# The branch to the general path is moved ahead of the last expert's last column group, and the planner restores its places after a skipped path

## The chip, the cores and the metric

The kernel runs on one core of a Trainium2 chip. The metric is the device time of one execution in microseconds (us). A core has TensorE (PE, matmuls; its weight loads are shown as PEld), VectorE (DVE), ScalarE (ACT), GpSimd (POOL) and SyncE (SP), each with its own instruction stream that it works through in order. Here SP issues nearly all transfers from HBM, and POOL does nothing but the branch.

## What is computed

A transformer of four layers on 256 tokens of width 1024, in float32. The first block has a convolution layer with a dense feed-forward, and an attention layer with a mixture of experts; the second block has two hybrid layers (three attention branches, the third over a memory `mem_2`) with an MLP each. The change lies in the mixture of experts and at the beginning of the first hybrid layer.

```python
def moe_swiglu(h, router, we_gate, we_up, we_down):
    logits = (h @ router).astype(jnp.float32)
    top_v, top_i = lax.top_k(logits, TOP_K)                  # 2 of 8 experts for each token
    ...
    for e in range(N_EXPERTS):
        out = out + gates[..., e:e + 1] * swiglu(h, we_gate[e], we_up[e], we_down[e])
    return out

def memory_attn(q, mem_n, w_mkv):
    kv = (mem_n @ w_mkv).reshape(B, M, 2, N_HEADS_M, HEAD_DIM)
    ...
```

## The kernel before

**Recording and planning.** The kernel's code does not issue instructions. It records them (`Recorder.add`), and `Recorder.flush` plans all that was recorded since the flush before and issues it. `issue` keeps a clock for each engine and for SP's queue, and picks at each step the instruction that could start first, by priority; loads have a large negative bias, so they come as early as a place for their tile is free. An engine's stream is fixed by this plan: if an instruction must wait on the chip for longer than the plan has it, all behind it on that engine waits too. All instructions therefore have the line of `op.fn` in the profile (L694 before, L695 after the change).

**Places.** SBUF has 28 "large" places (4 KB of each partition: weight tiles and their halves), 38 "gen" places (2 KB) and 20 small ones; PSUM has 8 banks. `Places.free` holds, in the planner's time, when each place is free, and `drop` sets it when a tile's last use is planned. What an instruction on the chip really waits for are semaphores, set by the tile framework from the program's text: the user before it of the same place. PE, ACT and DVE count their instructions up in a semaphore each, and SP's transfers share eight semaphores in turn, so at most eight are under way.

**The experts.** `route` gives each token its two experts and a position in each expert's list. The fast path has room for 96 tokens (`CAP`, three `BLOCKS` of 32) an expert. `experts()` goes over 32 steps, 8 experts with 4 column groups each. A step has `proj` (gate and up projections: tiles of `e_in`, 16 a step, 8 in the last group, which is half as wide), `act` (silu on ACT, product and transpose on DVE), and `down` of the step before (tiles of `e_down`, 8 a step, 4 for the last group). A tile is 128x1024 float32, 512 KB, and has 12 matmuls, which PE shows as 24 records. After an expert's last `down`, `scatter` adds its result to the activations `xT`: ACT and DVE split it in two halves, 12 pieces each, PE does 16 matmuls, DVE adds four tiles to `xT`.

**The branch.** `moe` (L1317) records all 32 steps and the load of the first two `c0_qk` weight tiles (`AHEAD`), holds what is still needed, and flushes. Then it loads the largest list length `most` into a register of every engine (L1326) and opens two nested branches (L1327 to L1331). In them all experts are gone over again for tokens beyond 96 and beyond 192, with a flush of their own. With these inputs no list is longer than 96, so the path is skipped: each engine compares, jumps, and adds to its semaphores what the skipped path would have added. `flush(aside=True)` sets the planner's engine clocks back, and lets no place be free later than the latest engine clock before the branch.

**Behind the branch** come, in one last flush: the scatter of expert 7; `fill(200)`, which runs `mem_second(1)`, the keys and values of `mem_2` for the second hybrid layer (4 tiles of `mem2T`, 2 of `c1_mk`, 2 of `c1_mv`; ACT squares and scales `mem2T`, PE does 16 matmuls of 128x256 in float32 for the keys and 16 for the values); the first hybrid layer `hybrid(0)`, whose first matmuls take `xT` and the 12 tiles of `c0_qk`, each split in two halves by ACT and DVE; and all the rest of the kernel.

Of the kernel before, what the change touches and what calls it, by code (L numbers as in the profile page):

```python
# [37 lines left out]
LATE = True  # L38
ATT_BIAS = 0
EARLY = 6  # L40
AHEAD = 1
LOAD_SHIFT = 0
Q_BIAS = 20e3
MEM1_BIAS = 20e3
MEM_AT = 2, 200
GATHER_AT = 1
GATES = 2
MEM_BIAS = (0, 0)
LOAD_FIRST = 1e9
SPLIT_LEAD = 5e3  # L50
# [290 lines left out]
class Recorder:  # L341
# [152 lines left out]
    def flush(self, aside=False):  # L494

        before = dict(self.free)
        ops, self.ops = self.ops, []
        if not ops:
            return
        self.issue(ops)  # L500
        if aside:
            self.free = before
            top = max(before.values())
            for op in ops:
                op.end = min(op.end, top)
            for c in self.kinds.values():
                for p in c.places:
                    p.free = [v if v is None else min(v, top) for v in p.free]
                for t in c.tiles:
                    t.end = min(t.end, top)  # L510

# [185 lines left out]
class Net:  # L697
# [493 lines left out]
    def down(self, acc, w, hh, hl, first, last):  # L1191
        for m in range(8):
            ms = slice(m * 128, (m + 1) * 128)
            for i, (wh, wl) in enumerate(w):
                self.mm3(acc[m // 2][:, (m % 2) * S:(m % 2 + 1) * S], (wh[:, 0, ms], wl[:, 0, ms]),
                         (hh[:, i], hl[:, i]), first and i == 0 and m % 2 == 0, last and i == 1, skip=True)
# [119 lines left out]

    def moe(self):  # L1317

        self.route()
        back, y = self.experts()  # L1320
        self.ahead = [self.load(self.a["c0_qk"][0, u]) for u in range(AHEAD)]
        held = [t for j in self.xn for p in j for t in p] + [self.pos, self.gate, back, y[0], y[2]]
        self.nc.hold(held)
        self.nc.hold([t for w in self.ahead for p in w for t in p])
        self.nc.flush()
        most = self.tc.nc.values_load(self.most[0:1, 0:1], min_val=0, max_val=S)  # L1326
        with ExitStack() as inner:  # L1327
            for base in range(CAP, S, CAP):
                inner.enter_context(self.tc.If(most > base))
                self.scatter(*self.experts(float(base)))  # L1330
                self.nc.flush(aside=True)  # L1331
        self.scatter(back, y)
        self.nc.release(held)
        self.fill(200)

    def onehot(self, e, base):
# [72 lines left out]
    def experts(self, base=0.0):  # L1409

        nc, a = self.nc, self.a
        steps = [(e, g) for e in range(NE) for g in range(GROUPS)]
        G, B, Y, T = {}, {}, {}, {}

        def prepare(e):
            oh = self.onehot(e, base)
            got = self.gather(oh)
            for i in range(2):
                G[e + i] = got[i]
                B[e + i] = self.back(oh, i, e + i)  # L1420

        def four(out, at, x, w, start, stop):
            for j in range(4):
                nc.tensor.matmul(out[32 * j:32 * j + 32, at:at + 256], x, w[:, 256 * j:256 * j + 256], start=start,
                                 stop=stop, skip_group_check=True)

        def proj(s):
            e, g = s
            p = [self.mm() for _ in range(BLOCKS)]
            for k in range(KT):  # L1430
                at = [48 + k] if g == GROUPS - 1 else [(g * KT + k) * 2, (g * KT + k) * 2 + 1]
                ws = [self.tile_of(a["e_in"][e, n]) for n in at]
                for b in range(BLOCKS):
                    for m, w in enumerate(ws):
                        four(p[b], m * 256, G[e][k][:, 32 * b:32 * b + 32], w, k == 0 and m == 0, k == KT - 1)
            return p

        def act(s, p):
            w = 128 if s[1] == GROUPS - 1 else 256
            T[s] = []  # L1440
            for b in range(BLOCKS):
                g = self.t([128, 256], F32, "eg")[:, :w]
                nc.scalar.activation(g, p[b][:, :w], AF.Silu)
                nc.vector.scalar_tensor_tensor(g, p[b][:, w:2 * w], B[s[0]][1][:, b:b + 1], g, op0=OP.mult, op1=OP.mult)
                t = self.t([128, 256], F32, "eh")
                nc.vector.transpose(t[:, :w], g)
                T[s].append(t)

        def down(s):
            e, g = s  # L1450
            if g == 0:
                y = [self.acc("y0"), self.acc("y1")]
                Y[e] = [y[0], y[0], y[1]]
            n = 4 if g == GROUPS - 1 else 8
            t = T.pop(s)
            for c in range(n):
                w = self.tile_of(a["e_down"][e, 8 * g + c])
                for b in range(BLOCKS):
                    four(Y[e][b], b % 2 * 256, t[b][:, 32 * c:32 * c + 32], w, g == 0 and c == 0 and b != 1,
                         g == GROUPS - 1 and c == n - 1)  # L1460
            if g < GROUPS - 1:
                return None
            y = Y.pop(e)
            return B.pop(e)[0], [y[b][:, b % 2 * 256:b % 2 * 256 + 256] for b in range(BLOCKS)]

        prepare(0)
        if not base:
            self.fill(2)
        for n, s in enumerate(steps):
            if not base:  # L1470
                self.fill(100 + n)
            act(s, proj(s))
            if n and (done := down(steps[n - 1])):
                self.scatter(*done)
            if s[1] == GATHER_AT and s[0] % 2 and s[0] + 1 < NE:
                prepare(s[0] + 1)
        return down(steps[-1])


    def fill(self, at):  # L1480
# [36 lines left out]
    def hybrid(self, l):  # L1517
        nc, a = self.nc, self.a
        f = self.feed(self.xT, "mix_g", l * 8)
# [4 lines left out]
        for c in range(3):  # L1524
            ps = [self.mm(), self.mm()]
            for u in range(2):
                if self.ahead:
                    w = self.ahead.pop(0)
                    self.nat(ps, f, w, 4 * u)
                    nc.release([t for p in w for t in p])  # L1530
                    continue
                w = self.load(a[f"c{l}_qk"][c, u])
                self.nat(ps, f, w, 4 * u)
            z = [self.t([128, 512], F32, f"z{j}") for j in range(2)]
# [20 lines left out]
        ps = [self.mm(), self.mm()]  # L1555
        for u in range(2):
            w = self.load(a[f"c{l}_v0"][0, u])
# [3 lines left out]
        w = self.load(a[f"c{l}_v1"])  # L1561
        p = self.mm()
# [3 lines left out]
        w = self.load(a[f"c{l}_qm"][0])  # L1566
        p = self.mm()
# [32 lines left out]
        kT, v = self.m2[l]  # L1600
# [5 lines left out]
        for mp in range(4):  # L1606
            w = self.load(a[f"c{l}_p"][mp])
            pp = []
            for ks in ([0], [1, 2, 3], [4, 5]):
                p = self.mm()  # L1610
                self.ws(p, w, ot, ks)
                pp.append(p)
            y = self.t([128, 2, S], F32, "y")
            t = self.t([128, 2, S], F32, "yt")
# [87 lines left out]
```

## Time and profile before

| | |
|---|---|
| three runs | 2177.43, 2179.4, 2180.08 us (median 2179.4) |
| profiled execution | 2182.62 us, its span 2180.8 us |
| PE busy | 2141.2 us, 98% of the span |
| DVE, ACT busy | 965.8 and 734.0 us |
| experts | about 440 to 1371 us |
| PE at the branch | 1370.1 us |

A timeline row has the start, the length, the engine, the instruction and in brackets the idle time before it with what ended it. A tile is named by its place (large, gen, bank) on the left of the arrow and by what is read on the right. A row of windows has the stretch, its length, each engine's busy time and number of instructions, the granted clock of PE (1 is full speed), the share of time that the transfer engines were busy, and GB/s. "Busy" on PE is modelled in parts, so idle time is taken from the gaps.

### The profile page before, as it was taken

How to read it: one execution, taken by the hardware profiler on the slowest of the kernel's cores; microseconds unless marked ns; L12 is line 12 of the kernel's file. 1: busy time of each engine (PE TensorE's matmuls, PEld its weight loads, DVE VectorE, ACT ScalarE, POOL GpSimd, SP SyncE). 2: the span in 40 equal slices, each digit the busy share in tenths (PEclk: the TensorE clock that was granted, in tenths of full speed). 3: DMA queues.
4: the chain of work that ended last, by engine and by line, in shares of the span. 5: the costliest groups of instructions: out<-in, count | busy, mean ns of one | idle time of the engine just before them, and what ended most of it. 6: DMA issues, size and time to landing. Idle time of an engine off the chain costs nothing. (4 is left out here: it accounts for less than half of the span.)

```text
span 2180.8 us, 57477 instructions
## 1 busy us (share of the span) xinstructions
PE 2141.2 (98%) x25496; PEld 1688.3 (77%) x25496; DVE 965.8 (44%) x2079; ACT 734.0 (34%) x1315; POOL 0.2 (0%) x4
## 2 busy tenths in 40 slices
PE   8999999999999999999999999899999999999998
PEld 8799997866565656656665656688999998899997
DVE  8975659510112011110302021666675566668553
ACT  8564547310101010010101010555554454655442
POOL 0000000000000000000000000000000000000000
PEclk9999999999999999999999999899999999999998
DMA  7445555489999999999899996653456555345550
GB/s 258 144 147 193 194 192 186 165 315 408 376 365 375 394 398 347 401 367 403 345 395 368 403 368 258 234 177 113 154 174 195 192 174 188 117 132 199 193 182 27
DMA packets 156209, 556.74 MB, mean 255 GB/s; under 512 B 17456, under 2 KB 20144, under 8 KB 155952
## 3 DMA queue, kind: packets, MB, share of 16 engines
q1 hardware_dynamic: 155952, 552.98, 69.3%
q8 instruction: 202, 3.31, 0.6%
q14 instruction: 55, 0.45, 0.1%
HBM read 551.87 MB, written 1.05 MB: 254 GB/s over the span
## 5 line engine op out<-in xcount | busy, mean ns | idle before, releaser
L694 PE MATMUL bank<-large,gen 128*32 128x256 f32 (+2 forms) x16896 | 1061.0, 380 | 0.0
L694 PE MATMUL bank<-gen,large 128*128 128x256 f32 x7468 | 943.3, 287 | 11.8 <-ACT large L694 8.1
L694 PEld LDWEIGHTS bank<-large,gen 128*32 128x32 f32 (+1 forms) x16896 | 656.7, 114 | 376.2 <-issue 6.1
L694 PEld LDWEIGHTS bank<-gen,large 128*128 128x128 f32 x7468 | 915.0, 190 | 29.8 <-issue 9.9
L694 DVE TENSOR_TENSOR large<-large,large 128x1024 fp32r<-128x1024 f32 (+1 forms) x356 | 429.6, 1210 | 129.4 <-PE bank L694 92.5
L694 ACT ACTIVATE gen<-bank 32x256 fp32r<-32x256 f32 (+7 forms) x322 | 124.2, 395 | 925.7 <-PE bank L694 897.8
L694 ACT ACTIVATE large<-large 128x1024 fp32r<-128x1024 f32 (+1 forms) x356 | 364.5, 1045 | 208.8 <-PE bank L694 120.6
L694 DVE SCALAR_TENSOR_TENSOR gen<-bank,small,gen 128x256 f32<-128x256 f32 (+2 forms) x100 | 44.3, 447 | 686.1 <-ACT gen L694 686.1
L694 ACT ACTIVATE gen<-gen 128x512 f32<-128x512 f32 (+3 forms) x149 | 89.6, 614 | 176.6 <-DVE gen L694 175.5
L694 DVE TENSOR_TENSOR gen<-bank,gen 32x256 fp32r<-32x256 f32 (+2 forms) x172 | 85.6, 505 | 138.9 <-ACT gen L694 73.4
L694 PE MATMUL bank<-gen,gen 128*128 128x192 f32 (+5 forms) x672 | 109.3, 341 | 11.8 <-ACT gen L694 7.3
L694 PEld LDWEIGHTS bank<-gen,gen 128*64 128x64 f32 (+3 forms) x672 | 68.3, 175 | 49.4 <-DVE gen L694 17.7
L694 DVE TENSOR_TENSOR gen<-gen,gen 128x512 f32<-128x512 f32 (+3 forms) x129 | 81.1, 637 | 50.2 <-ACT gen L694 48.4
L694 PE MATMUL bank<-ct,gen 128*128 128x128 f32 (+2 forms) x370 | 63.3, 275 | 7.1 <-DVE gen L694 6.8
L694 PEld LDWEIGHTS bank<-ct,gen 128*128 128x128 f32 (+1 forms) x370 | 45.2, 158 | 24.8 <-issue 13.2
L694 ACT ACTIVATE gen<-bank,small 128x256 f32<-128x256 f32 (+2 forms) x75 | 41.0, 569 | 50.5 <-PE bank L694 40.2
L694 DVE TENSOR_TENSOR xT<-xT,bank 128x512 f32<-128x512 f32 x64 | 43.6, 686 | 25.8 <-PE bank L694 24.8
L694 DVE SCALAR_TENSOR_TENSOR gen<-bank,gen 128x256 f32<-128x256 f32 (+1 forms) x66 | 25.4, 428 | 55.1 <-PE bank L694 54.5
L694 DVE SCALAR_TENSOR_TENSOR gen<-gen,pt,gen 128x256 f32<-128x256 f32 x108 | 43.3, 488 | 1.7 <-ACT gen L694 1.7
L694 DVE STREAM_TRANSPOSE gen<-gen 128x256 f32<-128x256 f32 (+1 forms) x96 | 38.7, 408 | 2.8
L694 ACT ACTIVATE gen<-gen,small 128x128 f32<-128x128 f32 x72 | 32.0, 448 | 17.8 <-DVE small L694 17.8
L694 DVE COPY small<-bank 32x1 f32<-32x1 f32 (+1 forms) x97 | 14.8, 152 | 46.6 <-ACT gen L694 44.9
(55 smaller groups left out, 374.2 us busy)
## 6 DMA issues: line engine op xcount, KB each, us to landing
large<-e_in SPq DMA_DIRECT2D x448, 512.0 KB, 6.9
large<-e_down SPq DMA_DIRECT2D x224, 512.0 KB, 6.8
large<-c_up SPq DMA_DIRECT2D x64, 512.0 KB, 4.4
large<-c_dn SPq DMA_DIRECT2D x64, 512.0 KB, 4.7
large<-c_g SPq DMA_DIRECT2D x48, 512.0 KB, 3.9
large<-c_qk SPq DMA_DIRECT2D x24, 512.0 KB, 5.9
large<-cv_gate SPq DMA_DIRECT2D x22, 512.0 KB, 4.5
large<-cv_up SPq DMA_DIRECT2D x22, 512.0 KB, 4.6
```

The costliest lines, as they stand in the source:

```text
L694: op.fn(*[real(x) for x in op.args], **{k: real(x) for k, x in op.kw.items()})
```

## The change

`experts()` becomes a generator. Ahead of step 31 (the last expert's last group; `LAST = 0` sets which) it yields the tiles that are still needed, `moe` holds them, flushes, makes the test and the skipped paths, and then lets the generator go on: step 31 with its `proj` and `act`, `down` of step 30, `down` of step 31 and the scatter are recorded behind the test, into the last flush. The load of two `c0_qk` tiles ahead of the test (`AHEAD`) is dropped. `flush(aside=True)` now sets each place's free time back to what it was before the skipped path.

```diff
@@ flush
         before = dict(self.free)
+        places = {p: list(p.free) for c in self.kinds.values() for p in c.places}
...
             for c in self.kinds.values():
                 for p in c.places:
-                    p.free = [v if v is None else min(v, top) for v in p.free]
+                    p.free = places[p]
@@ moe
         self.route()
-        back, y = self.experts()
-        self.ahead = [self.load(self.a["c0_qk"][0, u]) for u in range(AHEAD)]
-        held = [t for j in self.xn for p in j for t in p] + [self.pos, self.gate, back, y[0], y[2]]
-        self.nc.hold(held)
-        self.nc.hold([t for w in self.ahead for p in w for t in p])
-        self.nc.flush()
+        work = self.experts()
+        held = [t for j in self.xn for p in j for t in p] + [self.pos, self.gate] + next(work)
+        nc.hold(held)
+        nc.flush()
...
-                self.scatter(*self.experts(float(base)))
-                self.nc.flush(aside=True)
-        self.scatter(back, y)
-        self.nc.release(held)
+                for _ in self.experts(float(base)):
+                    pass
+                nc.flush(aside=True)
+        for _ in work:
+            pass
+        nc.release(held)
         self.fill(200)
@@ experts
+            if n == len(steps) - 1 - LAST:
+                e = s[0]
+                yield G[e] + list(B[e]) + [t for k in T for t in T[k]] + [Y[e][0], Y[e][2]]
             act(s, proj(s))
...
-        return down(steps[-1])
+        self.scatter(*down(steps[-1]))
@@ hybrid
-                if self.ahead:
-                    w = self.ahead.pop(0)
-                    self.nat(ps, f, w, 4 * u)
-                    nc.release([t for p in w for t in p])
-                    continue
```

In the rows below a tile's name has its place, then the tile's number; UNCONDITIONAL_BRANCH x3 is the end of the skipped paths, so that the row behind it is the first that runs after the test. SP's queue before, at the end of the skipped path (`waits` names the semaphores: PE_49, DVE_49 and Activation_49 are the engines' counts, DMAHW0 to 7 the eight of the transfers):

```order
L1327 UNCONDITIONAL_BRANCH [waits DMAHW0_49,DMAHW1_49,DMAHW2_49,DMAHW3_49,DMAHW4_49,DMAHW5_49,DMAHW6_49,DMAHW7_49] x2
L694 DMA gen3_37517<-mem2T 128x512 [waits DVE_49,DMAHW1_49,PE_49,Activation_49]
L694 DMA gen6_37523<-mem2T 128x512 [waits DMAHW2_49]
...
L694 DMA large0_37557<-c1_mk 128x1024 [waits DMAHW5_49]
...
L694 DMA large2_37587<-c1_mv 128x1024 [waits DMAHW7_49,DMAHW0_49]
...
L694 DMA large4_37608<-c0_qk 128x1024 [waits DMAHW1_49]
L694 DMA large5_37620<-c0_qk 128x1024 [waits DMAHW2_49]
```

And SP's queue after the change, at the same place; left out are seven rows of e_in, ten of e_down, and the later ones of mem2T, c1_mk, c1_mv and masks:

```order
L1327 UNCONDITIONAL_BRANCH [waits DMAHW0_49,DMAHW1_49,DMAHW2_49,DMAHW3_49,DMAHW4_49,DMAHW5_49,DMAHW6_49,DMAHW7_49] x2
L695 DMA large14_37205<-e_in 128x1024 [waits DMAHW7_49,DMAHW3_49,PE_49]
...
L695 DMA large0_37221<-e_down 128x1024 [waits DMAHW3_49,PE_49]
...
L695 DMA large27_37243<-e_down 128x1024 [waits DMAHW6_49,PE_49]
L695 DMA gen7_37245<-mem2T 128x512 [waits DVE_49,DMAHW7_49,PE_49,Activation_49]
...
L695 DMA large7_37541<-c0_qk 128x1024 [waits DMAHW4_49]
...
L695 DMA large7_37565<-c0_qk 128x1024 [waits DMAHW4_49,DMAHW0_49,DVE_49]
L695 DMA large9_37571<-c0_qk 128x1024 [waits DMAHW1_49,PE_49]
L695 DMA large0_37577<-c0_qk 128x1024 [waits DMAHW7_49,DMAHW2_49,DVE_49]
L695 DMA large7_37583<-c0_qk 128x1024 [waits DMAHW3_49,DMAHW0_49,DVE_49]
L695 DMA large5_37589<-c0_qk 128x1024 [waits PE_49]
```

Twenty expert tiles now stand between the branch and mem2T, and three of the c0_qk pieces share the place large7 (the second, sixth and ninth).

ACT before, behind the branch (32x256 are the scatter's splits out of PSUM, 128x512 the squares and 128x256 the scalings of mem2T, 128x1024 the splits of c0_qk):

```order
L1327 UNCONDITIONAL_BRANCH x3
L694 ACTIVATE gen0_37515<-bank5_15117 32x256 x2
L694 ACTIVATE gen0_37515<-bank6_15131 32x256
...
L694 ACTIVATE gen16_37548<-bank6_15131 32x256
L694 ACTIVATE gen18_37563<-gen3_37517 128x512
L694 ACTIVATE gen19_37570<-gen6_37523 128x512
L694 ACTIVATE gen3_37517<-gen3_37517,pt_67 128x256
...
L694 ACTIVATE large7_37681<-large4_37608 128x1024
```

ACT after the change (128x128 are the three silu of step 31; left out are four scaling rows and seven splits of c0_qk):

```order
L1327 UNCONDITIONAL_BRANCH x3
L695 ACTIVATE gen35_37255<-gen7_37245 128x512
L695 ACTIVATE gen22_37257<-gen15_37247 128x512
...
L695 ACTIVATE gen16_37251<-gen16_37251,pt_67 128x256 x2
L695 ACTIVATE gen25_37382<-bank1_37278 128x128
L695 ACTIVATE gen32_37389<-bank2_37285 128x128
L695 ACTIVATE gen29_37397<-bank3_37291 128x128
L695 ACTIVATE large18_37537<-large20_37535 128x1024
L695 ACTIVATE large14_37543<-large7_37541 128x1024
...
L695 ACTIVATE large0_37601<-large5_37589 128x1024
L695 ACTIVATE gen12_37614<-bank5_15117 32x256 x2
```

The scatter's splits stood first on ACT; now the squares and scalings of mem2T, the silu of step 31 and ten splits of c0_qk stand ahead of them. DVE has the same order with its parts of these.

PE after the change, from the last expert tile on (before, the scatter's sixteen matmuls, `gen,gen` 128x256 here, came straight behind the branch):

```order
L695 MATMUL bank5_15117<-large27_37243,gen8_37394 32x256 x4
L695 MATMUL bank5_15117<-large27_37243,gen6_37406 32x256 x4
L695 MATMUL bank6_15131<-large27_37243,gen37_37410 32x256 x4
L695 MATMUL bank0_37607<-ct_66,gen35_37255 128x1 x2
L695 MATMUL bank4_37610<-gen7_37245,large12_37253 128x256 x2
L695 MATMUL bank4_37610<-gen15_37247,large12_37253 128x256 x2
L695 MATMUL bank7_37631<-gen20_12611,gen12_37614 128x256
L695 MATMUL bank4_37610<-gen34_37249,large12_37253 128x256
```

Behind the branch PE now has 240 expert matmuls, then four key matmuls of the memory, and only then the scatter, mixed with the other key matmuls.

## Rows read from the trace of the kernel before

**Rows 1.** the page, part 1: busy us, share of the span, instructions

```profile
PE 2141.2 (98%) x25496; PEld 1688.3 (77%) x25496; DVE 965.8 (44%) x2079; ACT 734.0 (34%) x1315; POOL 0.2 (0%) x4
```

**Rows 2.** windows of 5 us around the branch, all engines

```profile
1370.00:1375.00 5.00, 1.19 (x20) 0.43 (x12) 0.26 (x1) 1.02 (x3) 0.00 (x0) 1.00 0.04 10
...
1375.00:1380.00 5.00, 2.94 (x9) 2.06 (x9) 3.22 (x8) 3.29 (x10) 0.00 (x0) 0.62 0.90 286
...
1380.00:1385.00 5.00, 3.69 (x10) 2.63 (x11) 4.67 (x10) 4.97 (x12) 0.00 (x0) 0.50 0.98 335
...
1390.00:1395.00 5.00, 5.00 (x17) 4.16 (x16) 4.90 (x16) 3.97 (x6) 0.00 (x0) 0.68 1.05 410
```

**Rows 3.** instructions of the branch's line L1327: ns min/median/max, first and last start

```profile
L1327 SPq EVENT_SEMAPHORE  x8: 17/17/17, 1344.5 to 1345.0; - x8
...
L1327 ACTq EVENT_SEMAPHORE  x1: 17/17/17, 1359.2 to 1359.2; - x1
...
L1327 DVEq EVENT_SEMAPHORE  x1: 21/21/21, 1362.0 to 1362.0; - x1
...
L1327 PEldq COMPARE_BRANCH  x1: 3682/3682/3682, 1370.1 to 1370.1; - x1
...
L1327 PEldq EVENT_SEMAPHORE  x1: 51/51/51, 1373.8 to 1373.8; - x1
```

**Rows 4.** timeline of SP's queue, the loads around the branch

```profile
1336.26 4.21 SPq L694 DMA_DIRECT2D large<-c_qk  x2
1373.94 2.53 SPq L694 DMA_DIRECT2D gen<-mem2T  x4
```

**Rows 5.** timeline of PE from the last expert tiles to the first c_qk matmul

```profile
1334.76 36.43 PE L694 MATMUL bank<-large,gen 128*32 128x256 f32 x668
...
1375.16 0.38 PE L694 MATMUL bank<-gen,gen 96*128 96x256 f32 x1 [3.97 <-ACT gen L694]
...
1384.68 2.76 PE L694 MATMUL bank<-gen,large 128*128 128x256 f32 x6
...
1395.90 4.48 PE L694 MATMUL bank<-large,gen 128*128 128x256 f32 x20
...
1403.60 5.58 PE L694 MATMUL bank<-large,gen 128*128 128x512 f32 x23
```

**Rows 6.** timeline of ACT and DVE around the branch

```profile
1354.83 0.28 ACT L694 ACTIVATE gen<-bank 128x128 f32<-128x128 f32 x1 [19.47 <-PE bank L694]
...
1355.53 0.31 DVE L694 STREAM_TRANSPOSE gen<-gen 128x128 f32<-128x128 f32 x1
...
1356.03 0.28 ACT L694 ACTIVATE gen<-bank 128x128 f32<-128x128 f32 x1 [0.43 <-PE bank L694]
...
1373.95 1.16 ACT L694 ACTIVATE gen<-bank 32x256 fp32r<-32x256 f32 x3 [15.74 <-PEq L1327]
...
1381.69 1.14 ACT L694 ACTIVATE gen<-gen 128x512 f32<-128x512 f32 x2
...
1382.73 2.89 ACT L694 ACTIVATE gen<-gen,pt 128x256 f32<-128x256 f32 x7
...
1390.82 2.94 ACT L694 ACTIVATE large<-large 128x1024 fp32r<-128x1024 f32 x3
...
1394.69 1.22 DVE L694 TENSOR_TENSOR large<-large,large 128x1024 fp32r<-128x1024 f32 x1
```

**Rows 7.** landing of c_qk loads (512 KB each); windows, behind the branch

```profile
DMA to landing us min/median/max: 3.7/5.9/10.7
...
1385.00:1400.00 15.00, 15.00 (x53) 12.31 (x53) 14.77 (x36) 11.93 (x20) 0.00 (x0) 0.73 1.03 404
```

**Rows 8.** another wait of PE and the granted clock behind it

```profile
1604.77 1.60 PE L694 MATMUL bank<-gen,large 128*128 128x256 f32 x6 [3.23 <-ACT gen L694]
...
1605.00:1608.00 3.00, 3.00 (x15) 3.00 (x16) 2.80 (x5) 2.33 (x4) 0.00 (x0) 0.50 0.00 0
...
1608.00:1611.00 3.00, 3.00 (x27) 3.00 (x26) 0.89 (x5) 0.32 (x1) 0.00 (x0) 0.95 0.57 175
```

More of the change, by code (lines that the diff above doesn't have):

```diff
@@ L40 @@
 EARLY = 6
-AHEAD = 1
 LOAD_SHIFT = 0
@@ L47 @@
 GATES = 2
+LAST = 0
 MEM_BIAS = (0, 0)
@@ L1317, in moe @@
     def moe(self):
+        nc = self.nc
         self.route()
-        back, y = self.experts()
-        self.ahead = [self.load(self.a["c0_qk"][0, u]) for u in range(AHEAD)]
-        held = [t for j in self.xn for p in j for t in p] + [self.pos, self.gate, back, y[0], y[2]]
-        self.nc.hold(held)
-        self.nc.hold([t for w in self.ahead for p in w for t in p])
-        self.nc.flush()
+        work = self.experts()
+        held = [t for j in self.xn for p in j for t in p] + [self.pos, self.gate] + next(work)
+        nc.hold(held)
+        nc.flush()
         most = self.tc.nc.values_load(self.most[0:1, 0:1], min_val=0, max_val=S)
```

## The prediction

> **What bounds the kernel now.** I read the page first: PE is busy for 98% of the span [rows 1], so time is lost only where PE stands still or runs at the low clock, and I went to the change's place with the table of short windows [rows 2]. From 1370 to 1375 us PE works 1.19 of 5 us, up to 1380 another 2.94 at a mean granted clock of 0.62 (1 is 2.4 GHz, 0.50 is 1.2), up to 1385 3.69 at 0.50; from 1390 to 1395 the mean is still only 0.68. The events of the branch's line say why [rows 3]: PE reaches COMPARE_BRANCH at 1370.1, is held 3682 ns, and posts its event semaphore at 1373.8; ACT, DVE and SP had done theirs by 1359.2, 1362.0 and 1345.0. SP's own queue [rows 4] shows the second fact: its last load before the branch was issued from 1336.26, its next one at 1373.94, 0.14 us behind PE's semaphore. SP had been free since 1345.0 and still waited for PE. So a load behind the branch does not start while PE is in front of it, if the tile's place was used in the skipped path. PE lived through those 30 us because the last tiles had landed by SP's semaphores from 1344.5 on [rows 3], 27 us ahead of PE's end.
>
> PE's own rows give the frame [rows 5]: the last expert matmul ends at 1334.76+36.43 = 1371.19, the first scatter matmul comes at 1375.16 after 3.97 idle, the first c_qk matmul (128x512) at 1403.60. That is 32.41 us from the one to the other.
>
> **The part that moves.** Step 31 is 8 e_in tiles and 4 e_down tiles; down of step 30, 8 tiles, also falls behind the test: 20 tiles, 240 matmuls. Their PE time: the third silu of step 31 starts at 1356.03 [rows 6], some 0.2 after PE's last proj matmul; the 144 matmuls left end at 1371.19, so 15.4/144 = 0.107 us each, 25.7 for 240. I count from Z, the end of PE's work before the test in its new place: Z = 1371.19 - 25.7 = 1345.5, and before, the first c_qk matmul stands at Z + 58.1. Everything behind it is the same work in nearly the same order, with PE full from 1403.60 on, so I take nothing gained or lost there (I allow -1.5 to +2). Now the same point after the change.
>
> 1. Branch. PE's semaphore comes 1373.8 - 1371.19 = 2.6 behind its last matmul, SP's first load 0.14 later: Z+2.75. In the new order all 20 tiles stand on SP behind the branch, and each waits for PE. In the built program PE's count is 10,915 at the branch, its semaphore behind the branch adds 16,704, and the first load waits for 27,279: no load can start earlier, whatever the planner believes of its place. The edit to flush changes that belief alone. The Trainium skill ("Advanced Engine Details and Errata", Control Flow Timing) gives a compare-and-branch about 108 ns; by that the first term would be 0.1 and the sum 2.5 shorter, but PE's row shows 3682 ns, so the row decides.
> 2. First tile. A 512 KB load took at least 3.7 us to land [rows 7]; at 404 GB/s [rows 7] 1.3 of that is transfer, 2.4 the fixed part. PE starts at Z+6.45 and gets a tile each 1.3: 16 tiles (proj of step 31, down of step 30) by Z+27.3, or some 1.7 later, since behind a wait of 3.23 us elsewhere PE ran 3 us at 0.50 and the next window has 0.95 [rows 8].
> 3. ACT. Its new order is the four mem2T squares and eight scalings, then the three silu of step 31. SP's order puts mem2T behind all 20 tiles: 10.49 MB at 404 GB/s is 26.0, so the last e_down lands at Z+2.75+2.4+26.0 = 31.1 and the first mem2T tile at 31.8. The twelve ACT instructions take 4 x 0.57 + 8 x 0.41 = 5.6 (1.14 for two, 2.89 for seven [rows 6]): Z+37.4. Silu, product, transpose and the signal took 1.0 in the trace (1354.83 to 1355.53+0.31) [rows 6], plus 0.2: PE begins down of step 31 at Z+38.6. It was ready by Z+29: about 10 us idle. The planner hid mem2T's work in front of silu because it takes mem2T as loaded long before; the cover is gone.
> 4. PE does those 4 tiles in 5 to 10 us (full or half clock): Z+44 to 49.
> 5. ACT and DVE again. Between silu and the first scatter split ACT's order now has ten splits of c_qk pieces. Behind the expert tiles SP sends 1.05 MB of mem2T, 2.10 of c_mk and c_mv, 0.79 of masks; the second c_qk piece lands at Z+5.15+15.47 MB/404 = 43.4. Its split takes 0.98 on ACT and 1.22 on DVE [rows 6], to 45.8. Piece 6 has the same place (large7) and waits for that DVE split: issued 45.9, landed 49.6, split by 51.95. Piece 9 waits for the same place again: issued 52.05, landed 55.75; piece 10 lands 1.3 behind it, 57.05, and ACT's split of it ends at Z+58.1. Only then come ACT's scatter splits. PE, done with step 31 and four memory matmuls by Z+46 to 52, waits for them: 7 to 13 us idle.
> 6. From ACT's first scatter split (1373.95) to the first c_qk matmul the trace has 29.65 [rows 5, 6]. Off this go the four memory matmuls done before, 0.92 each at the low clock (six records, two to a matmul, 2.76) [rows 5], or half of it at full clock, so 1.8 to 3.7; mem2T's ACT work is out of the way too. The upper bound is 27.8. The lower is the stretch without low clock: 1.2 to the first scatter matmul, 28 memory matmuls at 0.45 (twenty records in 4.48 [rows 5]), 12.5, the scatter's own waits, 3.4 as before, and some 4 for its 16 matmuls: 21. I take 24, between the two, since both shortenings act but PE comes out of a longer stop than in step 2. First c_qk matmul: Z+82.1.
>
> Sum: 82.1 - 58.1 = +24.0. Against the profiled execution (2182.62, span 2180.8) that is 2206.6; against the median of 2179.4 it is 2203.4. The gain that the change has by itself, the scatter laid among memory matmuls instead of alone behind the branch, is inside step 6.
>
> The bounds: step 6 gives -3 to +3.7; a load landing 1 us slower in steps 2 and 5 (three stand in line) +3; a rate 5 GB/s off adds or takes 0.3; behind c_qk -1.5 to +2. Together +19 to +32. The Trainium skill ("DMA: Bandwidth & Descriptors", Specifications) puts a core's HBM limit at about 358 GB/s; by that the 15.47 MB of step 5 would take 43.2 and the sum would be +29. The window of 15 us shows 404, so the row decides.
>
> **Rivals.** A, faster: SP passes the branch ahead of PE and fetches the 20 tiles while PE still computes. Then PE pays the branch alone and the scatter is covered by memory matmuls: of the 32.41 us go PE's idle parts from 1375 to 1385 (5-2.94 and 5-3.69, 3.4 [rows 2]) and up to 6.5 of low clock, so -3 to -10, near 2173. It decides by one point: the first e_in transfer behind the branch must start before PE's COMPARE_BRANCH. SP's 1373.94 and the counts speak against it: the change alters what the planner believes, not what the loads wait for. 4%.
> B, no change: SP waits but ACT does silu before mem2T is in. Then PE runs Z+6.45 to about 33.9 without a stop, and the rest is 32.41 less 3.97 of idle and 3.4 of scatter waits: Z+59, +1. The order of ACT speaks against it. 4%.
> C, slower still: the landing of loads behind the branch is nearer to the median than to the least of c_qk (5.9 against 3.7 [rows 7]), twice in step 5, +4.4, and PE stays at the low clock to the first c_qk matmul (27.8 in step 6, +3.8): +32, 2212. 17%.
> The forecast, two stops in place of one (+18 to +29): 75%.
>
> **Numbers.** Predicted 2203.4 us. The range is 2196 to 2213: it leaves out A and B, and the tails of the forecast and of C, some 15%. A difference of 0.2% (4.4 us) is about what a measurement can tell from none. Faster by more 4%, within it 4%, slower by more 92%.
>
> **What would show it.** In the profile after: SP's queue silent from about 28 us before PE's COMPARE_BRANCH until just behind its semaphore; then PE waits of about 4 us beyond the branch (for e_in), about 10 us (down of step 31, for DVE behind ACT), and 7 to 13 us (the scatter, for ACT), with the clock at 0.5 behind each. ACT's silu of step 31 right behind mem2T's scalings would show step 3, the gap between the landings of c_qk 6 and 9 step 5. A first e_in transfer ahead of PE's branch, or a silu ahead of mem2T, would show me wrong.

## The result

| | median of runs | profiled execution |
|---|---|---|
| before | 2178.9 us | 2182.62 us, span 2180.8 |
| after | 2203.54 us | 2202.52 us, span 2200.7 |

The changed kernel takes 1.0110 times as long as before (95% interval 1.0091 to 1.0129): 24.6 us more, where 24.0 were predicted (2203.4; range 2196 to 2213). A second set of runs of both kernels gave 1.0113 (1.0096 to 1.0130). The sum was right, and the two stops that it rests on are there. But its terms were off by 3 to 4 us in two directions, which nearly cancelled, and which of the two edits costs the time was settled only by the experiments.

### The profile after

PE's busy time on the page hardly moved [rows 1]: PE does the same work, and the loss is time in which it stands still or runs slowly.

```profile
PE 2139.4 (97%) x25496; PEld 1683.8 (77%) x25496; DVE 966.7 (44%) x2079; ACT 733.5 (33%) x1315; POOL 0.2 (0%) x4
```

The events of the branch's line (length in ns as min/median/max, then the first and the last start), as in [rows 3]:

```profile
L1327 SPq EVENT_SEMAPHORE  x8: 17/17/17, 1314.8 to 1317.3; - x8
...
L1327 SPq COMPARE_BRANCH  x1: 50/50/50, 1309.6 to 1309.6; - x1
...
L1327 PEldq COMPARE_BRANCH  x1: 3977/3977/3977, 1344.3 to 1344.3; - x1
L1327 PEldq EVENT_SEMAPHORE  x1: 51/51/51, 1348.3 to 1348.3; - x1
```

SP passes the branch at 1317.3, PE at 1348.3. SP's queue around it, as in [rows 4]:

```profile
1305.32 4.21 SPq L695 DMA_DIRECT2D large<-e_down  x4
1348.43 4.90 SPq L695 DMA_DIRECT2D large<-e_in  x8
1353.42 14.69 SPq L695 DMA_DIRECT2D large<-e_down  x12
1369.09 5.18 SPq L695 DMA_DIRECT2D gen<-mem2T  x4
```

From 1309.53 to 1348.43 SP issues no load, and the first one comes 0.1 us behind PE's semaphore: the twenty expert tiles wait for PE although SP has been free for 31 us. PE's timeline (start, length, engine, instruction, in brackets the idle time before it with what ended it), as in [rows 5]:

```profile
1304.68 40.75 PE L695 MATMUL bank<-large,gen 128*32 128x256 f32 x748
1352.53 21.19 PE L695 MATMUL bank<-large,gen 128*32 128x256 f32 x360 [7.10 <-DMA large<-e_in]
1373.91 1.50 PE L695 MATMUL bank<-large,gen 128*32 128x256 f32 x24 [0.19 <-DMA large<-e_down]
1386.17 7.18 PE L695 MATMUL bank<-large,gen 128*32 128x256 f32 x96 [10.76 <-DVE gen L695]
...
1408.40 0.58 PE L695 MATMUL bank<-gen,gen 96*128 96x256 f32 x1 [12.67 <-ACT gen L695]
...
1428.16 3.50 PE L695 MATMUL bank<-large,gen 128*128 128x512 f32 x14
```

Z, the end of PE's work before the test, is 1304.68+40.75 = 1345.43. Before there was one stop at this place, 3.97 us [rows 5]; now there are three, 7.10, 10.76 and 12.67. ACT's timeline, as in [rows 6], shows who holds PE in the second and the third:

```profile
1379.74 1.25 ACT L695 ACTIVATE gen<-gen 128x512 f32<-128x512 f32 x2 [44.25 <-DMA gen<-mem2T]
...
1382.34 2.88 ACT L695 ACTIVATE gen<-gen,pt 128x256 f32<-128x256 f32 x7
1385.13 0.58 ACT L695 ACTIVATE gen<-bank 128x128 f32<-128x128 f32 x3
1390.21 1.06 ACT L695 ACTIVATE large<-large 128x1024 fp32r<-128x1024 f32 x1 [4.50 <-DMA large<-c_qk]
...
1397.78 1.06 ACT L695 ACTIVATE large<-large 128x1024 fp32r<-128x1024 f32 x1 [1.42 <-DMA large<-c_qk]
...
1405.00 1.06 ACT L695 ACTIVATE large<-large 128x1024 fp32r<-128x1024 f32 x1 [2.41 <-DMA large<-c_qk]
...
1407.21 2.77 ACT L695 ACTIVATE gen<-bank 32x256 fp32r<-32x256 f32 x7
```

ACT stands for 44.25 us in front of mem2T's first square. The silu of step 31 (128x128 at 1385.13) come right behind mem2T's scalings, and PE's second stop ends 1 us later. Then ten c_qk splits (1390.21 to 1406.25) precede the first scatter split (32x256 at 1407.21), and PE's third stop ends 1.2 us behind that. The clock, in windows as in [rows 2] (PE's busy time is the first number behind the length, its granted clock the one behind POOL's):

```profile
1380.00:1385.00 5.00, 0.00 (x0) 0.00 (x0) 2.50 (x4) 5.00 (x12) 0.00 (x0) 0.50 1.03 403
1385.00:1390.00 5.00, 3.83 (x40) 1.78 (x44) 1.57 (x6) 0.71 (x4) 0.00 (x0) 0.51 1.05 402
...
1410.00:1415.00 5.00, 4.97 (x15) 3.36 (x15) 3.55 (x8) 2.69 (x7) 0.00 (x0) 0.50 0.63 244
1415.00:1420.00 5.00, 5.00 (x22) 4.27 (x22) 4.46 (x12) 2.77 (x8) 0.00 (x0) 0.78 0.35 108
1420.00:1425.00 5.00, 5.00 (x25) 4.41 (x24) 4.93 (x19) 1.91 (x5) 0.00 (x0) 1.00 0.32 105
```

Behind the second and the third stop PE comes back at 0.50, 1.2 GHz, and behind the third it is at full clock again from 1420 on.

### The profile page after: what moved, and what is told of

Read it like the earlier page. It is cut to its first block, busy times and chain, and to the rows that moved or that the text cites. A ratio compares the mean times of both kernels' runs of the same rounds, so it can differ in the third digit from the quotient of the medians.

```text
span 2200.7 us, 57477 instructions
## 1 busy us (share of the span) xinstructions
PE 2139.4 (97%) x25496; PEld 1683.8 (77%) x25496; DVE 966.7 (44%) x2079; ACT 733.5 (33%) x1315; POOL 0.2 (0%) x4
## 5 line engine op out<-in xcount | busy, mean ns | idle before, releaser
L695 PE MATMUL bank<-large,gen 128*32 128x256 f32 (+2 forms) x16896 | 1064.6, 380 | 18.1 <-DVE gen L695 10.8
L695 PEld LDWEIGHTS bank<-gen,large 128*128 128x128 f32 x7468 | 911.8, 190 | 27.8 <-issue 9.9
L695 PE MATMUL bank<-ct,gen 128*128 128x128 f32 (+2 forms) x370 | 61.8, 271 | 7.1 <-DVE gen L695 6.9
L695 PEld LDWEIGHTS bank<-ct,gen 128*128 128x128 f32 (+1 forms) x370 | 43.6, 152 | 24.6 <-issue 13.8
```

Source lines behind the costliest of these rows:

```text
L695: op.fn(*[real(x) for x in op.args], **{k: real(x) for k, x in op.kw.items()})
```

## The experiments

The change has two parts: the test is moved, and the planner gets each place back as it was before the skipped path. Three causes stood against each other. **Theory:** the planner takes the loads behind the test as done early, so it writes mem2T's and c_qk's work into ACT's and DVE's streams ahead of work for which PE waits; on the chip these streams then wait for the loads. **Rival 1:** the emptied queue alone, twenty tiles that can be fetched only behind PE's branch, whatever the order. **Rival 2:** the move of the test by itself. Each experiment's ratio is to runs of before on the same chip.

### One part at a time: e1_old_places and e2_places_only

```diff
e1_old_places, against the changed kernel:
-        places = {p: list(p.free) for c in self.kinds.values() for p in c.places}
-                    p.free = places[p]
+                    p.free = [v if v is None else min(v, top) for v in p.free]
e2_places_only, against the kernel before:
+        places = {p: list(p.free) for c in self.kinds.values() for p in c.places}
-                    p.free = [v if v is None else min(v, top) for v in p.free]
+                    p.free = places[p]
```

> The changed kernel with the old line of flush put back (a place is free no later than the latest engine clock ahead of the test), so that the move of the test stands alone. Theory: the cost sits in the streams of ACT and DVE, which the plan fills with mem2T's and c_qk's work ahead of silu of step 31 and ahead of the scatter's splits because it believes their loads done early. With the old belief these orders should turn: the stops of 10.8 us (down of step 31, for DVE) and 12.7 us (scatter, for ACT) vanish, the stop of 7.1 us for e_in stays, and the scatter has waits of some 3 us as before the change: 2203.5 - 23.4 + 3.4 = 2183.5, or 2 to 4 less with the low clock behind the two stops gone; 2179 to 2185. Rival 1, the emptied load queue alone is the cause: the loads still all wait for PE, so it stays at 2199 or more. Rival 2, the move of the test by itself: also 2199 or more.

> The kernel before with the edit to flush alone: the test stays behind step 31, the places are restored. Theory: the planner now thinks mem2T, c_mk, c_mv and the c_qk pieces loaded long before the test, while on the chip they start at PE's semaphore (1373.8 in the trace of before). ACT's stream behind the test then has c_qk splits ahead of scatter's splits, as in the changed kernel, and PE stops for the loads: mem2T lands some 7 us behind the branch, and the tenth split ends at least two places' chains (4 + 4 us) behind the landing of 1.05 + 2.10 + 0.8 MB; one or two stops of 10 to 16 us, 2190 to 2202. Rival 2, the move of the test is the cause: no change, 2177 to 2181. Rival 1, the emptied queue: SP's queue is as empty as in before, no change, 2177 to 2181.

Measured: the move alone takes 1.0019 times as long (1.0005 to 1.0032), which is 4.1 us of 2179.03; by the medians it is 6.5 (2185.56, just above the 2179 to 2185 expected). The restored places alone take 1.0085 (1.0066 to 1.0104), 19.3 us by the medians (2198.35, inside the 2190 to 2202 expected). PE's timeline with the move alone:

```profile
1352.38 22.00 PE L694 MATMUL bank<-large,gen 128*32 128x256 f32 x360 [6.44 <-DMA large<-e_in]
1374.72 6.77 PE L694 MATMUL bank<-large,gen 128*32 128x256 f32 x120 [0.34 <-DMA large<-e_down]
1383.98 0.67 PE L694 MATMUL bank<-gen,large 128*128 128x256 f32 x2 [2.49 <-ACT gen L694]
```

The wait for e_in is there (6.44); those of 10.8 and 12.7 are gone, with 2.49 in place of the latter. In the kernel with the restored places alone the test stands where it stood before, and SP's queue is no emptier than before (mem2T issued from 1374.22, before from 1373.94 [rows 4]). Yet PE stops for 11.26 and for 17.26 us:

```profile
1382.47 0.99 PE L695 MATMUL bank<-ct,gen 128*128 128x1 f32 x4 [11.26 <-DVE gen L695]
1400.71 0.58 PE L695 MATMUL bank<-gen,gen 96*128 96x256 f32 x1 [17.26 <-ACT gen L695]
```

Its ACT timeline has the cause of both: PE's first matmuls behind the branch now need mem2T's squares, which ACT can start only when mem2T lands, and seven c_qk splits, each waiting for its load, stand ahead of the scatter's.

```profile
1377.61 1.26 ACT L695 ACTIVATE gen<-gen 128x512 f32<-128x512 f32 x2 [19.39 <-DMA gen<-mem2T]
...
1388.79 1.06 ACT L695 ACTIVATE large<-large 128x1024 fp32r<-128x1024 f32 x1 [4.60 <-DMA large<-c_qk]
...
1399.54 2.31 ACT L695 ACTIVATE gen<-bank 32x256 fp32r<-32x256 f32 x6
```

So of the 24.6 us some 19 belong to the line in `flush` and 4 to 6 to the move, and the two nearly add up. Rival 2 falls, except for the small part that the move does cost. Rival 1 can't be the whole either.

### The order alone: e3_sp_clock

```diff
+        nc.free["SP"] = max(nc.free.values()) + 2700
         for _ in work:
             pass
```

> The changed kernel, places restored as in it, and one line more: behind the skipped paths the planner's clock of SP is set to the latest engine clock plus 2.7 us, which is what the trace shows (first load 2.9 us behind PE's last matmul). Nothing on the chip is changed but the order that the plan writes. Theory: the orders of ACT and DVE turn as in the run with the old line, the two stops of 10.8 and 12.7 us go, the stop of 7.1 us for e_in stays: 2179 to 2185. Rival 1 (the emptied queue alone) and rival 2 (the move alone): 2199 or more, since loads and test stand where they stood.

Measured: 2181.87 us, 1.0010 times before (1.0000 to 1.0020). One line that tells the planner when its loads can start gives back 22 of the 24.6 us: the test, the restored places and the loads' waits for PE are as in the changed kernel, only the written plan differs. PE's two stops go, that for e_in stays:

```profile
1351.56 28.57 PE L695 MATMUL bank<-large,gen 128*32 128x256 f32 x480 [6.91 <-DMA large<-e_in]
1382.59 1.40 PE L695 MATMUL bank<-gen,large 128*128 128x256 f32 x4 [2.45 <-DMA large<-c_mk]
```

This separates the cause from rival 1: the emptied queue explains the 6.91, not the rest. Two things are not separated. The plan is more than the order on ACT and DVE: it also hands out other places, and SP issues the twelve c_qk loads from 1379.05 to 1395.93 here, from 1382.98 to 1407.66 in the changed kernel, so the pieces that there wait for one another's place do so no longer. And the profiled execution (2178.6) is one of the fastest of its ten. The dropped early load of two c_qk tiles was not tried by itself; here it is dropped too, and ACT's first c_qk split, at 1390.33, waits for no load.

### The wait itself: e6_res16, e7_res16_belief, e10_res16_late12

Sixteen large places are kept out of the skipped path, so that the tiles behind the test share no place with it. `reserve` takes them and makes the planner's limits smaller by 16, `give` puts them back:

```diff
+        some = nc.reserve(16)
         most = self.tc.nc.values_load(...)
...
+        nc.give(16, some, 2700)      # e6_res16; 12000 in e10_res16_late12
         for _ in work:
             pass
@@ give; the loop is left out in e7_res16_belief
+        at = max(self.free.values()) + late
+        for c in self.kinds.values():
+            for p in c.places:
+                p.free = [v if v is None else max(v, at) for v in p.free]
+        for v, i in some:
+            self.kinds["raw"].places[0].free[i] = v
```

> A version that would take the wait itself away: in the changed kernel 16 of the 28 large places are kept out of the skipped path (it must do with 12), so that loads into them behind the test wait for no engine's skipped count; the planner is told that all other places come free 2.7 us behind the latest engine clock. Theory: SP issues e_in into the 16 places as soon as it has passed the test itself, some 28 us ahead of PE's compare-and-branch; PE then pays the branch alone (2.9 us and a short clock loss) instead of 7.1, 10.8 and 12.7. The kernel before lost 3.97 idle at the branch, 3.4 in the scatter's waits and up to 6.5 at the low clock; of this some 3 at the branch stay: 2170 to 2176, faster than both. Rival: SP is held by PE for another reason than the places (its first load again just behind PE's semaphore): then PE waits 7.1 us for e_in as in the changed kernel, 2179 to 2185.

> The 16 kept places as in e6_res16, but the planner is not told that the other places come free late: it believes of mem2T's, c_mk's and c_qk's loads what it believed in the changed kernel. Theory (two separate prices, an emptied queue and a plan whose order does not fit the landings): the stop of 7.1 us for e_in shrinks to 2.9, the stop of 10.8 us at down of step 31 goes, since mem2T (issued just behind PE's semaphore, not behind 20 tiles) is squared and scaled before step 31 ends; but ten c_qk splits still stand ahead of the scatter's splits on ACT, so a stop of 7 to 12 us stays there. 2203.5 - 4.2 - 10.8, and up to 4 less at the low clock: 2184 to 2190. Rival (the emptied queue alone costs the time): as in e6_res16, 2174 to 2178.

> As e6_res16, but the planner takes the places that are not kept as free 12 us behind the latest engine clock, not 2.7. In e6_res16 a stop of 3.33 us was left ahead of the scatter, with seven c_qk splits in front of the scatter's splits on ACT, because SP's queue behind PE's semaphore lands them some 9 us later than planned. Theory: the splits of the scatter move ahead of c_qk's, the stop shrinks to 1 us or less and the low clock behind it with it: 2 to 4 us less than e6_res16, 2172 to 2174. Rival (ACT's order does not set it): 2175 to 2177.

Measured: e6_res16 2176.0 us, 0.9985 (0.9975 to 0.9995); e7_res16_belief 2181.68, 1.0020 (1.0011 to 1.0030); e10_res16_late12 2174.6, 0.9986 (0.9977 to 0.9996). The first and the last beat both kernels, by some 3 us against before. SP's queue and PE in e6_res16:

```profile
1312.88 9.44 SPq L716 DMA_DIRECT2D large<-e_in  x8
1324.10 8.57 SPq L716 DMA_DIRECT2D large<-e_down  x8
1350.70 2.80 SPq L716 DMA_DIRECT2D gen<-mem2T  x4
...
L1349 SPq COMPARE_BRANCH  x1: 50/50/50, 1332.7 to 1332.7; - x1
```

```profile
1350.72 27.74 PE L716 MATMUL bank<-large,gen 128*32 128x256 f32 x478 [2.91 <-PEq L1349]
...
1382.87 0.39 PE L716 MATMUL bank<-gen,gen 96*128 96x256 f32 x1 [3.33 <-ACT gen L716]
...
1403.04 3.52 PE L716 MATMUL bank<-large,gen 128*128 128x512 f32 x14
```

The sixteen tiles are issued from 1312.88 on, and PE waits for the branch alone (2.91). One thing went otherwise than expected: SP's compare-and-branch stands at 1332.7 in this kernel, behind these loads. They do not pass the test early, they no longer stand behind it. So this run shows what the waiting tiles cost; it does not show whether a load into a kept place that stands behind the test would pass ahead of PE.

e7_res16_belief has the loads early and the wrong belief. The stops for e_in and at down of step 31 are gone, one of 8.85 us stays at the scatter, behind ten c_qk splits on ACT:

```profile
1388.23 0.58 PE L712 MATMUL bank<-gen,gen 96*128 96x256 f32 x1 [8.85 <-ACT gen L712]
```

The time came out 2.3 us below the 2184 to 2190 expected and 3.7 above the 2174 to 2178 of rival 1. What decides is the stop at the scatter, 8.85 against 3.33 in e6_res16, and the two intervals, which lie apart: an early load does not repair an order that still waits for later loads. In e10_res16_late12 PE's timeline has

```profile
1379.66 0.39 PE L716 MATMUL bank<-gen,gen 96*128 96x256 f32 x1
...
1400.29 3.50 PE L716 MATMUL bank<-large,gen 128*128 128x512 f32 x14
```

The stop of 3.33 us at the scatter is gone, as the theory had it, but not the time that was to go with it: from PE's semaphore to the first c_qk matmul it takes 1400.29-1348.4 = 51.9 us, e6_res16 1403.04-1350.6 = 52.4, and the two ratios are the same; the median is above the 2172 to 2174 expected. PE comes to the scatter later instead: step 31 ends 30.4 us behind the semaphore (1378.78), in e6_res16 27.8 (1378.39). There the windows have the clock at 0.50 from 1350 to 1355 and at 0.84 from 1355 to 1360, in e6_res16 at 0.66 and 1.00. PE also stood for 0.71 us at 1350.86. So ACT's order sets the stop, but in this execution the stretch behind the branch, most of it at the low clock, took back what it gave; whether it does so in each was not tried.

### Steps 3 and 5 apart: e4_mem_early_after

```diff
-MEM_AT = 2, 200
+MEM_AT = 2, 108
```

> The changed kernel with one number changed: the memory of the second hybrid layer (mem2T, c_mk, c_mv, 3.15 MB) is done among the first experts, ahead of the test. It tries steps 3 and 5 of the prediction apart. Theory: nothing of mem2T stands ahead of silu of step 31, so the stop of 10.8 us there goes wholly; the tenth split of c_qk comes 3.15 MB / 404 = 7.8 us earlier, but PE has 5 us of down and 7 to 9 us of memory matmuls less to do in front of the scatter, so the stop there grows from 12.7 to 13 to 17. First c_qk matmul some 7 to 9 us earlier behind Z; 2194 to 2198. Rival (the stops are the emptied queue's): 2201 to 2206, as in the changed kernel.

Measured: 2199.88 us, 1.0103 (1.0085 to 1.0121), 22.4 us over before, 2.2 less than the changed kernel; its four runs go from 2196.41 to 2203.07, two of them within the 2194 to 2198 expected, the other two within the rival's 2201 to 2206. So the time alone decides nothing; the stops do. PE's timeline:

```profile
1367.56 27.77 PE L695 MATMUL bank<-large,gen 128*32 128x256 f32 x480 [6.89 <-DMA large<-e_in]
1411.53 0.58 PE L695 MATMUL bank<-gen,gen 96*128 96x256 f32 x1 [16.20 <-ACT gen L695]
```

The stops are as expected: with no mem2T in front of silu that of 10.8 us is gone altogether (the 480 records run through), and that at the scatter has grown, from 12.67 to 16.20. How much of that reaches the end stays open, with runs so far apart. What the rows show is that the memory's matmuls are not saved: they now lie ahead of the test, whose place moves from 1345.43 to 1367.56-6.89 = 1360.67, and behind the stop the scatter has less to lie among. The expectation for the first c_qk matmul left this out: 7 to 9 us earlier behind Z were expected, and 26 were measured (1417.17-1360.67 = 56.5 against 82.73). In this run, taking one stop away leaves the other to wait for the same loads: the scatter starts when ACT has the tenth split done.

### The floor: e9_no_branch

```diff
-        most = self.tc.nc.values_load(self.most[0:1, 0:1], min_val=0, max_val=S)
-        with ExitStack() as inner:
-            for base in range(CAP, S, CAP):
...
-                nc.flush(aside=True)
```

> The changed kernel without the test and without the general path (left out: tokens beyond 96 an expert, of which these inputs have none). It gives the floor: what the test in its new place costs in all. Theory: no stop at the branch, for e_in, at down of step 31 or ahead of the scatter, and the scatter lies among memory matmuls; the kernel before loses 3.97 + 3.4 us idle and up to 6.5 at the low clock at its branch, so 2179 - 7.4 = 2171.6 down to 2165. Rival (the stops have another cause than the loads behind the test, for example the order of the scatter and the memory): stops of several us stay at the scatter, 2176 or more.

Measured: 2169.46 us, 0.9961 (0.9946 to 0.9975). PE runs through step 31 without a stop, with 1.24 us at the scatter:

```profile
1289.70 82.19 PE L695 MATMUL bank<-large,gen 128*32 128x256 f32 x1516
...
1375.50 0.39 PE L695 MATMUL bank<-gen,gen 96*128 96x256 f32 x1 [1.24 <-ACT gen L695]
```

Against this floor the kernel before is 8.0 us longer (2177.5 on that chip), e10_res16_late12 5.1 (2174.6). What its rows show of these 5.1 is PE's own: 3.19 us idle at the branch, then the low clock (0.50 from 1350 to 1355).

### Both kernels again: b_again and a_again

In the first two profiles the stretch behind the first c_qk matmul took 2180.8-1403.60 = 777.2 us before and 2200.7-1428.16 = 772.5 after, although the same work stands there.

> The kernel before once more, for a second profiled execution. In the first, from the first c_qk matmul to the end took 777.2 us against 772.5 in the changed kernel, while the medians differ by what the two differ at the first c_qk matmul (24.6). If that is the plan (a wait of 3.23 us for ACT 201 us behind c_qk, and the low clock behind it, which the kernels with restored places don't have), the stretch takes 776 to 778 again. If it was that execution, the wait is under 1 us and the stretch takes 773 to 774.

> The changed kernel once more, for a second profiled execution and a second interval beside that of the kernel before. The stretch behind the first c_qk matmul took 772.5 us; if that is the plan, 772 to 774 again. The stops of 7.1, 10.8 and 12.7 us come back within 1 us each, and step 6 (from ACT's first scatter split to the first c_qk matmul) takes 20 to 22, not the 24 that was predicted: if it does, the term was mis-sized and not a chance of one execution.

Measured: b_again 2176.15 us, 0.9997 (0.9987 to 1.0006); a_again 2202.94. The stretch takes 2174.3-1401.77 = 772.5 and 2200.0-1428.19 = 771.8. PE's wait of 3.23 us for ACT [rows 8] shrank to 0.50 in the second execution of the same program, so it was that execution and no part of the plan:

```profile
1401.77 5.58 PE L694 MATMUL bank<-large,gen 128*128 128x512 f32 x23
...
1582.22 21.72 PE L694 MATMUL bank<-gen,large 128*128 128x256 f32 x178 [0.50 <-ACT gen L694]
```

The changed kernel's three stops came back as 6.44, 10.75 and 13.26 us, and step 6 took 1428.19-1407.71 = 20.5. In the kernel before, the same stretch, from ACT's first scatter split to the first c_qk matmul, took 1401.77-1374.60 = 27.2 in the second execution, against 29.65 in the first [rows 5, 6]: its clock was 1.00 from 1390 to 1395, against 0.68 [rows 2].

## What the runs add up to

| against before, by the medians | the planner believes the loads early | the planner knows them late |
|---|---|---|
| test moved, all places shared with the skipped path | +24.6 (the change) | +2.8 (e3_sp_clock) |
| test moved, 16 places kept | +4.2 (e7_res16_belief) | -3.0 (e6_res16) |
| no test, nothing late | | -8.0 (e9_no_branch) |

The medians are of different chips, each set against before on its own, with an interval of some 2 us either way. Down the right column: the emptied queue costs 2.8+3.0 = 5.8, and what is left of the test with the places kept 5.0. Across the first line: the wrong belief costs 21.8; across the second, 7.2. The rows say why it is less: in e7_res16_belief mem2T is issued right behind PE's semaphore and lands while PE works through step 31, so one stop is left of two. In e2_places_only, where mem2T is issued as early but PE has no expert work behind the test, it costs 19.3. As far as these runs go, a wrong order costs what PE has no other work to cover.

## Why the prediction was right, step by step

| step, behind Z | predicted | measured |
|---|---|---|
| 1: SP's first load | 2.75 | 3.00 |
| 2: PE starts, 16 tiles done | 6.45; 27.3 to 29.0 | 7.10; 29.98 |
| 3: first mem2T tile, ACT's twelve, down of 31 | 31.8; +5.6; 38.6 | 34.3; +5.5; 40.74 |
| stop in step 3 | about 10 | 10.76 |
| 4: four tiles | 5 to 10 us | 7.18 us |
| 5: pieces 6 and 9 on ACT, first scatter split | 49.6; 55.75; 58.1 | 52.35; 59.6; 61.8 |
| stop in step 5 | 7 to 13 | 12.67 |
| 6: to the first c_qk matmul | 24 | 20.95 |
| first c_qk matmul | 82.1 | 82.73 |

**Right:** SP's silence (34.8 us ahead of PE's COMPARE_BRANCH, where some 28 were named, to just behind its semaphore), the order of ACT, the two stops and what ends them. Rival A falls by the row it named: the first e_in load comes behind PE's compare-and-branch. Rival B falls by ACT's order. Rival C came near the lateness of the scatter's splits (4.4, measured 3.7) but put it all in step 5's landings, where 1.1 of it was, and it had the low clock to the end. The counts of PE's semaphore in step 1 stand in no row; the row that bears on them is SP's first load, 0.1 us behind PE's semaphore. The upper bounds add up to +33, not +32; the range of 2196 to 2213 holds that too.

**Step 3's term was mis-sized by 2.5 us.** The rate holds: the windows above have 403 and 402 GB/s from 1380 to 1390, and 404 was taken [rows 7]. What the sum left out is that loads under way are moved side by side. The first mem2T tile is in 31.3 us behind SP's first load; 10.75 MB at 404 GB/s, up to and with that tile, make 26.6 of that, and 4.7 are left where 2.4 were taken from the least landing of a c_qk load [rows 7]. But in this stretch 380 GB/s for 31.2 us, 11.86 MB, were moved, so 1.1 MB of the loads issued behind the tile came in ahead of its end: 2.8 us of the 4.7. The mem2T loads took 7.7 to 10.6 us each to land. The other 1.9 us, no more than the fixed part taken, fit the start of the empty queue, with a mean of 224 GB/s in the first window:

```profile
1348.00:1353.00 5.00, 0.47 (x8) 0.30 (x12) 0.00 (x0) 0.00 (x0) 0.00 (x0) 0.59 0.70 224
1348.50:1379.70 31.20, 22.69 (x384) 13.42 (x384) 0.00 (x0) 0.00 (x0) 0.00 (x0) 0.89 0.99 380
...
DMA to landing us min/median/max: 7.7/9.7/10.6
```

The Trainium skill ("DMA: Bandwidth & Descriptors", Specifications) has about 358 GB/s for a core; the windows of 403 and 402 are past it, as that of [rows 7] was.

**Step 5's chain was mis-sized by 1.1 more.** From piece 6 on ACT to piece 9 on ACT, split, DVE's split, issue and landing, the trace takes 1405.00-1397.78 = 7.2; 6.15 was put together from the least landing, 3.7. With step 3's 2.5 carried along, that makes nearly all of the 3.7 us by which the scatter's splits came late.

**Step 6 was mis-sized by 3.05 the other way,** and this hid the other two. The prediction chose 24 between 21 and 27.8, with PE at the low clock for long. The lower bound had 3.4 of waits inside the scatter and no low clock. In the trace it is the other way round: PE is at 0.50 until 1415 and below full clock until 1420, but busy for 4.97 of 5 us from 1410 on, since the memory's matmuls fill the scatter's gaps. So the lower bound was reached, by other terms than its own, in both executions (20.95 and 20.5). And the 29.65 that the step started from was 27.2 in the second execution of before, so 2.5 of it was the clock of one execution. In the second pair of executions the end of step 6 differs by 1428.19-1401.77 = 26.4 us, the medians by 26.8. A point forecast that comes within 0.2 us of the median owes that to luck; that the stops add some 25 us is not luck.

**What the prediction left out.** It said that the edit to `flush` "changes that belief alone", which is so, and then priced the order only as a consequence of the moved loads. The belief alone, with nothing moved, costs 19. And "the gain that the change has by itself", inside step 6, does not show in the time: with the order repaired (e3_sp_clock) the moved test is still no faster than before, with PE idle for 6.91 us at the branch where it was 3.97. A time below that of before is had only with the places kept.

## What to carry to other kernels

Where a plan writes the order of in-order engines, an estimate that is too early for one load can cost more than the load's own delay: everything behind the first instruction that needs it stands, on an engine for which others wait. Read behind a branch first when each queue issues its next load and which engine's semaphore it waited for, and give the planner that time before moving any work. To take the wait away, let what comes next use places that the skipped path does not touch; in e6_res16 this put the loads ahead of the test.

## What the runs showed of the hardware

The compare-and-branch over the skipped path takes 50 ns on SP and ACT and 72 on DVE by its own row, but 3397 to 3977 ns on PE in the eleven runs that have the test. On the other engines the time stands behind it: in the changed kernel ACT's is at 1335.6 and its semaphore at 1338.2, DVE's at 1336.7 and 1339.5, SP's at 1309.6 and 1314.8. So 2.6, 2.8 and 5.2 us pass on these engines until the next row, and only PE shows such a time in the row's length. What the engines do in that time no row says. The Trainium skill ("Advanced Engine Details and Errata", Control Flow Timing) gives about 108 ns for it; the rows of SP, ACT and DVE are a half to two thirds of it, and the time to the next instruction is over twenty times as long on each.

```profile
L1327 ACTq COMPARE_BRANCH  x1: 50/50/50, 1335.6 to 1335.6; - x1
L1327 DVEq COMPARE_BRANCH  x1: 72/72/72, 1336.7 to 1336.7; - x1
L1327 ACTq EVENT_SEMAPHORE  x1: 17/17/17, 1338.2 to 1338.2; - x1
L1327 DVEq EVENT_SEMAPHORE  x1: 21/21/21, 1339.5 to 1339.5; - x1
```
